# One straight program for each expert, with small conditional parts, in place of three arms

## The chip, the cores and the metric

The kernel runs on one core of a Trainium2 chip. The metric is the device time of one execution in microseconds (us). Each engine (TensorE, VectorE, ScalarE, GpSimd, SyncE) has an instruction stream of its own, and they wait for one another by semaphores. [...]

## What is computed

One layer on 256 tokens of 1024 channels: three token mixers, then a mixture of 32 experts of which each token takes four. The change touches the experts alone:

```python
def _moe(t, router_w, router_b, w_gu, b_gu, w_dn, b_dn):
    logits = (t @ router_w + router_b).astype(jnp.float32)
    top_vals, top_idx = lax.top_k(logits, TOP_K)
    gates = jax.nn.softmax(top_vals, axis=-1).astype(t.dtype)
    ...
    def expert_block(args):
        xe, e = args
        h = xe @ w_gu[e] + b_gu[e]
        gate, up = h[:, :D_FF], h[:, D_FF:]
        gate = jnp.minimum(gate, SWIGLU_LIMIT)
        up = jnp.clip(up, -SWIGLU_LIMIT, SWIGLU_LIMIT)
        return ((up + 1) * (gate * jax.nn.sigmoid(SWIGLU_ALPHA * gate))) @ w_dn[e] + b_dn[e]
```

Each expert holds 1024 x 2048 gate/up weights and 1024 x 1024 down weights in 32-bit floats, 12 MiB. How many tokens an expert has is known only when the kernel runs. With the inputs used here three experts (2, 15, 17) have over 64 tokens (84 at most), ten (3, 6, 7, 10, 12, 18, 24, 25, 30, 31) have 33 to 64, and the other nineteen 32 or fewer.

## The kernel before

The mixers run up to about 400 us, then the 32 experts one after another, then the final normalisation. Each expert's weights are twelve tiles of 1 MiB, `wt[0]` to `wt[7]` for gate/up (one for each 128 input channels) and `wt[8]` to `wt[11]` for down. They are loaded by SyncE into a ring of 19 slots, each as soon as the tile that held the slot has been read for the last time; the first 19 are loaded while the mixers still run.

The tokens of an expert are picked out of the 256 by a matmul with a one-hot matrix (`gather`), transposed to channels on partitions (`spread_rows`), multiplied with the weights, and put back by a second one-hot matmul (`scatter`, with the one-hot `sc` that VectorE makes from `pbr`) whose result VectorE adds to the accumulator `acc` (L1126). The product of the down weights is first multiplied with the gate (`weigh`: ScalarE L1115 makes the rounded part `yh`, then VectorE L1116 the rest `yl`). Two jobs are shared between neighbouring experts. `flush(prev)` is the scatter of the expert before: eight matmuls into four tiles, four additions. `fill` prepares the tokens of the next pair of experts, 64 places for each: an even expert gathers them (eight matmuls), an odd one transposes them (eight transposes).

An expert is one of three arms, chosen by its count in registers that each engine loads (L1294) and compares (L1337, L1338):

- `tiny`, up to 32 tokens: four groups of 32 array columns work side by side on four quarters of a weight tile (`pGU..t`, L1178 bias, L1183 gate/up, L1191 down bias, L1203 down).
- `light`, 33 to 64: two groups of 64 columns (L1139 bias, L1144 gate/up, L1162 down).
- `heavy`, over 64: a gather of its own for 128 places (L966) and all 128 columns (L1239, L1265).

In `tiny` and `light` TensorE's order is that of the code. After the second weight tile (`if k == 1`) stands the flush for an even expert and the transposes of fill for an odd one; after the down bias, beside the gate chain (`swiglu`: VectorE L1079, ScalarE L1081, VectorE L1083 to L1085), stands the other of the two. Then follow the turn of the gate product (`turned`, L1092, ScalarE L1094) and the down matmuls. Small results lie in four PSUM buffers with one tag (`sm`). Ahead of the last expert, 31, stands a jump (L1329) over code for experts with over 128 tokens, which doesn't run here, and an early flush of expert 30.

Of the kernel before, what the change touches and what calls it, by code (L numbers as in the profile page):

```python
# [29 lines left out]
TINY = 32  # L30
LIMIT = 7.0
# [109 lines left out]
def _consts():  # L141
# [26 lines left out]
    slot = np.full((P, 6), -5.0)  # L168
    slot[:64, 0] = p[:64] + 1
    slot[64:, 1] = p[:64] + 1  # L170
    slot[:, 2] = p + 1
    slot[:, 3] = p + 1 + P
    slot[:64, 4] = p[:64] % TINY + 1
    slot[64:, 5] = p[:64] % TINY + 1
# [8 lines left out]
def tile_trunk(ctx, tc, xT_d, xn_d, wf_d, vec_d, row_d, rw_d, cst_d, cst2_d, rope_d, ln1_d, ln2_d,  # L183
# [688 lines left out]
    cnt = mo.tile([P, NE + 1], I32, name="cnt")  # L872
    idr = mo.tile([P, P], F32R, name="idr")
# [122 lines left out]
    with tc.manual_schedule():  # L996
# [41 lines left out]
        V.tensor_copy(cnt[96:P, 0:NE], prk[1][96:P])  # L1038
        cmx = ch.tile([P, 1], F32, name="cmx")
# [30 lines left out]
    def sm(name, shape=None):  # L1070
        return pse.tile(shape or [P, 512], F32, tag="sm", name=name, bufs=4)

    def quarter(w, h, q):

        return w.rearrange("p (g n) -> p g n", g=2)[:, :, h * 512 + q * 256:h * 512 + (q + 1) * 256]

    def swiglu(ps, name):
# [4 lines left out]
        uv = ex.tile([P, 256], F32, tag="uv", name=f"uv{name}", bufs=2)  # L1082
# [14 lines left out]
    def gate_slots(lhs, e, name):  # L1097
# [6 lines left out]
        gsl = ex.tile([P, 1], F32, tag="gsl", name=f"gsl{name}", bufs=2)  # L1104
# [3 lines left out]
    def scatter_lhs(e, slots, sc, name):  # L1108
        pbr = sm(f"pbr{name}", [P, S])
        T.matmul(pbr, idr[:, e:e + 1].to_broadcast([P, P]), rankT, start=True, stop=True)  # L1110
        for i, s_ in enumerate(slots):
            V.tensor_scalar(sc[:, i], pbr, C("slot", s_, s_ + 1), None, op0=ALU.is_equal)  # L1112
# [5 lines left out]
    def scatter(c, n, sc, ys, name):  # L1118
        po = sm(f"pos{name}{c}{n}")
        ls = sc[:, c * P:(c + 1) * P]  # L1120
        w = 512 // len(ys)
        for i, (yh, yl) in enumerate(ys):
            T.matmul(po[:, i * w:(i + 1) * w], ls, yh, start=True, stop=False)  # L1123
            T.matmul(po[:, i * w:(i + 1) * w], ls, yl, start=False, stop=True)  # L1124
# [3 lines left out]
    def flush(prev):  # L1128
        if prev:
            e, sc, yh, yl = prev  # L1130
            for c in range(2):
                for n in range(2):
                    scatter(c, n, sc[:, n], [(yh, yl)], f"{e}")

    def light(e, oh, xg, bl, wt, prev, cur, fill):
        s_ = slice((e % 2) * CAP, (e % 2 + 1) * CAP)
        ps = [bank(2 + q, f"pGU{e}{q}") for q in range(2)]
        for q in range(2):
            T.matmul(ps[q], bl, bgu_t[:, q * 512:(q + 1) * 512], start=True, stop=False)  # L1139
        _, sc, yh, yl = cur  # L1140
        for k in range(KT):
            for q in range(2):
                for h in range(2):
                    T.matmul(ps[q][h * 64:(h + 1) * 64].rearrange("p (g n) -> p g n", g=2), xg[:, k, s_],  # L1144
                             quarter(wt[k], h, q), start=False, stop=(k == KT - 1))
            if k == 1:
                fill("l") if e % 2 else flush(prev)
            if k == 5:
                gsl = gate_slots(lambda c: oh[:, c, e % 2], e, f"{e}")
        pY = bank(0, f"pY{e}")  # L1150
        T.matmul(pY, bl, bdn_t, start=True, stop=False)
        uv = [swiglu(ps[q], f"{e}_{q}") for q in range(2)]
        flush(prev) if e % 2 else fill("l")
        scatter_lhs(e, (0, 1), sc, f"{e}")
        pT = bank(1, f"pT{e}", [P, 2, 2, P])
        hT = [turned(uv[q], f"{e}_{q}", pT[:, q]) for q in range(2)]
        for b in range(2):
            for h in range(2):
                for j in range(2):
                    lhs = hT[b][:, j, h * CAP:(h + 1) * CAP]  # L1160
                    for n in range(2):
                        T.matmul(pY[n * 64:(n + 1) * 64], lhs, wt[KT + 2 * b + h][:, j, n * 512:(n + 1) * 512],  # L1162
                                 start=False, stop=(b == 1 and h == 1 and j == 1))
        weigh(pY, gsl, yh, yl)

    def tiny(e, oh, xg, bl, wt, prev, cur, fill):


        nm = f"{e}t"
        ps = bank(2, f"pGU{nm}")  # L1170
        quarters = [(h, q) for h in range(2) for q in range(2)]
        _, sc, yh, yl = cur

        def grp(t, g):
            return t[g * TINY:(g + 1) * TINY]

        for g, (h, q) in enumerate(quarters):
            T.matmul(grp(ps, g), bl[:, g * TINY:(g + 1) * TINY].bitcast(F32),  # L1178
                     bgu_t[:, q * 512:(q + 1) * 512].bitcast(F32), start=True, stop=False)
        lo = (e % 2) * CAP  # L1180
        for k in range(KT):
            for g, (h, q) in enumerate(quarters):
                T.matmul(grp(ps, g).rearrange("p (g n) -> p g n", g=2), xg[:, k, lo:lo + TINY],  # L1183
                         quarter(wt[k], h, q), start=False, stop=(k == KT - 1))
            if k == 1:
                fill("t") if e % 2 else flush(prev)
            if k == 5:
                gsl = gate_slots(lambda c: oh[:, c, e % 2, 0:TINY], e, nm)
        pY = bank(0, f"pY{nm}")
        for n in range(2):  # L1190
            T.matmul(grp(pY, 2 * n), bl[:, n * CAP:n * CAP + TINY].bitcast(F32), bdn_t.bitcast(F32),  # L1191
                     start=True, stop=False)
        uv = swiglu(ps, nm)
        flush(prev) if e % 2 else fill("t")
        scatter_lhs(e, (4, 5), sc, nm)
        hT = turned(uv, nm, bank(1, f"pT{nm}", [P, 2, P]))
        for b in range(2):
            for h in range(2):
                g = 2 * h + b
                last_ = (b, h) == (1, 1)  # L1200
                for j in range(2):
                    for n in range(2):
                        T.matmul(grp(pY, 2 * n + j), hT[:, j, g * TINY:(g + 1) * TINY],  # L1203
                                 wt[KT + 2 * b + h][:, j, n * 512:(n + 1) * 512],
                                 start=(j == 1 and (b, h) == (0, 0)), stop=last_)
        weigh(pY, gsl, yh, yl)

    def heavy_onehot(e, part):
        oh = ex.tile([P, 2, P], F32R, tag=("ohx", "sg")[part], name=f"ohx{e}h{part}", bufs=2)
        for c in range(2):  # L1210
            V.tensor_scalar(oh[:, c], C("iota_s"), rank[c][:, e:e + 1], -float(part * P),
# [3 lines left out]
    def heavy_gather(e, part, ohx):  # L1215
# [5 lines left out]
        for i in range(4):  # L1221
            r = ex.tile([P, 256], F32, tag=("gv", "uv")[i % 2], name=f"raw{nm}{i}", bufs=2)
# [4 lines left out]
    def heavy(e, part, ohx, wt, prev, cur, fill=None):  # L1227
        nm = f"{e}h{part}"
        if fill and e % 2:
            fill("h")  # L1230
# [6 lines left out]

        def gu(k, h, q):
# [263 lines left out]
```

## Time and profile before

| | us |
|---|---|
| median of three runs | 1440.43 (1439.58 to 1445.16) |
| the profiled execution | 1446.26 |
| its span | 1444.4 |
| TensorE busy | 1139.7 (79%) |
| VectorE busy | 622.1 (43%) |
| ScalarE busy | 322.8 (22%) |
| GpSimd busy | 294.1 (20%) |

The span counts from the first to the last instruction of the profiled execution. Busy time says what an engine spent in operations, not what held up the end; for that one reads what an engine waited for and where its idle time lies. "Issue" as a releaser means that the engine waited for nothing that the profile shows, and an engine's name with a q stands for its sequencer, which handles branches and semaphores.

### The profile page before, as it was taken

The page shows a single profiled execution, that of the slowest core. Times are in us where ns is not written, and L with a number is a line of the kernel's source. Part 1 is how long each engine was busy: PE and PEld are TensorE (multiplying, and loading weights), DVE is VectorE, ACT ScalarE, POOL GpSimd, SP SyncE. Part 2 cuts the span into 40 slices and gives each one's busy share as a digit, 9 for nine tenths or more (in the row PEclk, how much of TensorE's full clock was granted, in tenths as well). Part 3 has the DMA queues.
Part 4 walks back from the last instruction along what each step waited for, and adds up shares of the span by engine and source line. Part 5 has one row for each costly group of instructions (what it writes and reads, how often), then busy time and mean ns, then how long its engine had stood idle before and what let it go on. Part 6 is the DMA issues. An engine that isn't in the chain of part 4 may idle for free. (4 is left out here: it accounts for less than half of the span.)

```text
span 1444.4 us, 18035 instructions
## 1 busy us (share of the span) xinstructions
PE 1139.7 (79%) x6902; PEld 635.4 (44%) x6902; DVE 622.1 (43%) x1289; ACT 322.8 (22%) x651; POOL 294.1 (20%) x293
## 2 busy tenths in 40 slices
PE   8797696899965998778597859869978678766666
PEld 8686586899722442233132325334322233221223
DVE  5999996876642232224222323313232312232203
ACT  5465463654411111011010101111100101100001
POOL 5999999533120000000000000000000000000000
PEclk9998788999888999899798979979999989999778
DMA  7243333477869689999999999966999999999950
GB/s 248 100 146 117 113 133 108 159 237 271 334 234 415 262 341 413 415 415 413 415 415 416 414 413 409 363 260 262 416 413 415 415 415 415 414 414 416 415 231 29
DMA packets 89524, 456.79 MB, mean 316 GB/s; under 512 B 8304, under 2 KB 8704, under 8 KB 58496
## 3 DMA queue, kind: packets, MB, share of 16 engines
q1 hardware_dynamic: 89344, 454.33, 79.6%
q8 instruction: 120, 1.97, 0.6%
q14 instruction: 60, 0.49, 0.1%
HBM read 453.25 MB, written 1.05 MB: 315 GB/s over the span
## 5 line engine op out<-in xcount | busy, mean ns | idle before, releaser
L1391 POOL TENSOR_TENSOR xn<-xn,lb 128x256 f32<-128x256 f32 x4 | 2.8, 726 | 1027.1 <-DVE xn L1379 1027.1
L1144 PE MATMUL pGU<-ew,xg 128*64 128x512 f32 x640 | 159.4, 649 | 0.7 <-issue 0.7
L1126 DVE TENSOR_TENSOR xn<-xn,pos 128x512 f32<-128x512 f32 x124 | 77.1, 680 | 134.0 <-issue 116.1
L393 POOL TENSOR_TENSOR cbc<-cbc,ups 128x256 f32<-128x256 f32 x120 | 123.4, 1029 | 4.6
L248 DVE TENSOR_TENSOR wl<-raw,wh 128x1024 fp32r<-128x1024 f32 (+1 forms) x72 | 99.9, 1394 | 37.3 <-ACT wh L247 37.1
L247 ACT CAST wh<-raw 128x1024 fp32r<-128x1024 f32 (+1 forms) x89 | 91.0, 1030 | 57.0 <-DMA raw<-in_wf_dram 23.4
L392 POOL TENSOR_TENSOR ups<-ups,vec 128x256 f32<-128x256 f32 x120 | 102.2, 871 | 0.0
L1144 PEld LDWEIGHTS pGU<-ew,xg 128*64 128x64 f32 x640 | 46.7, 149 | 95.9 <-issue 94.2
L1162 PE MATMUL pY<-ew,hT 128*64 128x512 f32 x320 | 75.1, 624 | 0.0
L1139 PE MATMUL pGU<-bgu_t,bl 128*128 128x512 f32 x20 | 10.9, 643 | 75.4 <-issue 74.7
L1081 ACT ACTIVATE sg<-gv 128x256 f32<-128x256 f32 x20 | 8.3, 417 | 224.2 <-DVE gv L1079 224.2
L1123 PE MATMUL pos<-yh,sc 128*128 128x512 f32 x124 | 52.8, 426 | 1.7 <-DVE yl L1116 1.7
L248 POOL TENSOR_TENSOR wl<-raw,wh 128x1024 fp32r<-128x1024 f32 x17 | 42.2, 2488 | 52.1 <-ACT wh L247 40.5
L1124 PE MATMUL pos<-yl,sc 128*128 128x512 f32 x124 | 48.8, 394 | 0.0
L1162 PEld LDWEIGHTS pY<-ew,hT 128*64 128x64 f32 x320 | 23.1, 144 | 45.1 <-issue 44.4
L1116 DVE SCALAR_TENSOR_TENSOR yl<-pY,gsl,yh 128x512 fp32r<-128x512 f32 x10 | 7.5, 750 | 80.4 <-ACT yh L1115 80.4
L1139 PEld LDWEIGHTS pGU<-bgu_t,bl 128*128 128x128 f32 x20 | 4.6, 287 | 82.7 <-issue 82.7
L1123 PEld LDWEIGHTS pos<-yh,sc 128*128 128x128 f32 x124 | 23.3, 188 | 29.0 <-issue 21.9
L403 DVE SCALAR_TENSOR_TENSOR xacc<-xp,vec,xacc 128x256 f32<-128x256 f32 x48 | 35.6, 746 | 0.5
L1105 DVE COPY gsl<-pgs 128x1 f32<-128x1 f32 x10 | 1.6, 158 | 76.8 <-PE pgs L1103 76.8
L291 PE MATMUL px<-xh,wh 128*128 128x256 f32 x96 | 29.9, 312 | 5.9 <-ACT pt L553 4.8
L293 PE MATMUL px<-xh,wl 128*128 128x256 f32 x96 | 28.9, 301 | 0.4 <-DVE wl L248 0.4
(1235 smaller groups left out, 2567.4 us busy)
## 6 DMA issues: line engine op xcount, KB each, us to landing
ew<-in_wgu_dram SPq DMA_DIRECT2D x241, 1024.0 KB, 19.9
ew<-in_wdn_dram SPq DMA_DIRECT2D x124, 1024.0 KB, 19.4
raw<-in_wf_dram SPq DMA_DIRECT2D x87, 512.0 KB, 3.6
ew<-in_wgu_dram SPq DMA_DIRECT2D x30, 512.0 KB, 6.3
ew<-in_wdn_dram SPq DMA_DIRECT2D x8, 512.0 KB, 5.7
xraw<-in_xT_dram SPq DMA_DIRECT2D x4, 256.0 KB, 5.1
xn<-in_xn_dram SPq DMA_DIRECT2D x2, 512.0 KB, 6.7
lnt<-in_ln_dram SPq DMA_DIRECT2D x2, 512.0 KB, 10.1
```

What stands on the lines that cost most here:

```text
L247: A.copy(h[:, b], raw[:, b])
L248: (PO if u in LOW_POOL else V).tensor_sub(l[:, b], raw[:, b], h[:, b].bitcast(F32))
L291: T.matmul(ps, wh, mh(k), start=(k == 0), stop=False)
L293: T.matmul(ps, wl, mh(k), start=False, stop=(k == nk - 1))
L392: PO.tensor_tensor(pr, up[:, j:j + S], W("cw31", c * 31 + j).to_broadcast([P, S]), op=ALU.mult)
L393: PO.tensor_add(acc, acc, pr)
L403: V.scalar_tensor_tensor(acc, xp[:, j:j + S], W("cw5", t * 5 + j), acc, op0=ALU.mult, op1=ALU.add)
L1123: T.matmul(po[:, i * w:(i + 1) * w], ls, yh, start=True, stop=False)
L1124: T.matmul(po[:, i * w:(i + 1) * w], ls, yl, start=False, stop=True)
L1126: V.tensor_add(dst, dst, po)
L1144: T.matmul(ps[q][h * 64:(h + 1) * 64].rearrange("p (g n) -> p g n", g=2), xg[:, k, s_], quarter(wt[k], h, q), start=False, stop=(k == KT - 1))
L1162: T.matmul(pY[n * 64:(n + 1) * 64], lhs, wt[KT + 2 * b + h][:, j, n * 512:(n + 1) * 512], start=False, stop=(b == 1 and h == 1 and j == 1))
```

## The change

The three arms give way to one function, `expert`. Each expert is now up to two groups: `many` is true over 32 tokens and runs the first 64 places as two groups of 64 columns, `four` is true up to 32 and over 64 and runs one group of 32 places as four groups of 32 columns (the expert's only tokens, or places 65 to 96), `over` is true over 64. The flags are computed on VectorE for all experts at once; each engine loads three of them into registers for each expert. The work is cut into parts, each in a conditional of its own: the second gather, gate/up of two weight tiles at a time, the gate chain, the turn, down of two weight tiles at a time, the middle scatter, and the weighting. On TensorE these are 18 conditionals for an expert, on ScalarE and VectorE nine each. A part that is left out is a taken branch to one instruction that waits until TensorE (or the engine it is on) has finished all that stands ahead, and then raises the engine's semaphore by the part's count.

The scatter takes 64 of the 128 partitions for each half of the channels and one scatter one-hot in place of two. The small PSUM tiles have three buffers in place of four. The fallback now covers experts with over 96 tokens (`TOP`), which do not occur here, and stays as a jump ahead of expert 31.

```diff
+    flag = mo.tile([P, 3, NE], I32, name="flag")
+    base = mo.tile([P, NE], F32, name="base")
...
+        pn = mm("pn", [P, NE])
+        for c in range(2):
+            T.matmul(pn, C("ones"), Pm[c], start=(c == 0), stop=(c == 1))
+        V.tensor_scalar(base, pn, float(CAP), float(CAP), op0=ALU.is_gt, op1=ALU.mult)
+        V.tensor_scalar(flag[:, 0], pn, float(TINY), None, op0=ALU.is_gt)
+        V.tensor_scalar(flag[:, 1], pn, float(CAP), None, op0=ALU.is_gt)
+        V.scalar_tensor_tensor(flag[:, 2], pn, float(TINY), flag[:, 1], op0=ALU.is_le, op1=ALU.add)
...
     def sm(name, shape=None):
-        return pse.tile(shape or [P, 512], F32, tag="sm", name=name, bufs=4)
+        return pse.tile(shape or [P, 512], F32, tag="sm", name=name, bufs=3)
...
+    def scatter(pos, c, sc, ys, start=True):
+
+        for i, y in enumerate(ys):
+            for n in range(2):
+                r = slice(n * 64, (n + 1) * 64)
+                T.matmul(pos[n], sc[r, c * P:(c + 1) * P], y[r], start=(start and i == 0), stop=(i == 1))
...
+    def expert(e, oh, xg, bl, wt, prev, cur, fill):
+
+
+        many, over, four = [[nc.values_load(flag[0:1, i, e:e + 1], engines=g, min_val=0, max_val=1,
+                                            skip_runtime_bounds_check_because="comparisons of a count")
+                             for g in ((ENG.PE,), (ENG.Activation, ENG.DVE))] for i in range(3)]
...
+        first, second = (fill, lambda: flush(prev)) if e % 2 else (lambda: flush(prev), fill)
+
+        def on(cond, *parts):
+
+            for c_, f in zip(cond, parts):
+                if f:
+                    with tc.If(c_):
+                        with pe_order():
+                            f()
...
+        xs_ = ex.tile([P, KT, TINY], F32, tag="xsm", name=f"xsm{e}", bufs=1)
+        A.copy(xs_, xg[:, :, lo:lo + TINY])
+        pg = bank(1, f"pgs{e}", [P, KT, TINY])
...
+        on(over, gather_more, copy_more)
+        pL = [bank(2 + q, f"pGL{e}{q}") for q in range(2)]
+        pS = bank(4, f"pGS{e}")
+
+        def up_many(k0):
...
+            for k in (k0, k0 + 1):
+                for q in range(2):
+                    for h in range(2):
+                        T.matmul(pL[q][h * 64:(h + 1) * 64].rearrange("p (g n) -> p g n", g=2),
+                                 xg[:, k, s_], quarter(wt[k], h, q), start=False, stop=(k == KT - 1))
+
+        def up_four(k0):
...
+            for k in (k0, k0 + 1):
+                for g, (h, q) in enumerate(QUARTERS):
+                    T.matmul(grp(pS, g).rearrange("p (g n) -> p g n", g=2), xs_[:, k],
+                             quarter(wt[k], h, q), start=False, stop=(k == KT - 1))
+
+        for k0 in range(0, KT, 2):
+            on(many, lambda: up_many(k0))
+            on(four, lambda: up_four(k0))
+            if k0 == 0:
+                with pe_order():
+                    first()
+        uv = [gate_tiles(f"{e}_{q}") for q in range(2)]
+        on(many, None, lambda: [swiglu_into(uv[q], pL[q]) for q in range(2)])
+        uv.append(gate_tiles(f"{e}_2"))
+        on(four, None, lambda: swiglu_into(uv[2], pS))
+        with pe_order():
+            second()
...
+        on(many, turn_many, turned_many)
+        on(four, turn_four, turned_four)
...
         for b in range(2):
+            on(many, lambda: down_many(b))
+            on(four, lambda: down_four(b))
+        on(many, None, lambda: weigh(pY[0], gsl[0], yh, yl))
+        for c in range(2):
+            pos = [sm(f"pom{e}{c}{n}") for n in range(2)]
+            on(over, lambda: scatter(pos, c, sc, (yh, yl)), lambda: [add(c, n, pos[n]) for n in range(2)])
+        pb2 = sm(f"pbs{e}", [P, S])
+        on(four, lambda: T.matmul(pb2, idr[:, e:e + 1].to_broadcast([P, P]), rankT, start=True, stop=True),
+           lambda: (slots(sc, pb2, 1, e), weigh(pY[1], gsl[1], yh, yl)))
...
-            with tc.If(count(NE, ALL) > P):
+            with tc.If(count(NE, ALL) > TOP):
...
-        rv = count(e, (ENG.PE, ENG.Activation, ENG.DVE))
-        with tc.If(rv > TINY) as some:
-            with tc.If(rv > CAP) as cond:
-                heavy(e, 0, ohx, wt, prev, cur, fill)
-            with cond.Else():
-                with tc.manual_schedule(engines={mybir.EngineType.PE}):
-                    light(e, oh, xg, bl, wt, prev, cur, fill)
-        with some.Else():
-            with tc.manual_schedule(engines={mybir.EngineType.PE}):
-                tiny(e, oh, xg, bl, wt, prev, cur, fill)
+        expert(e, oh, xg, bl, wt, prev, cur, fill)
```

The order of the built program differs from that of the code in one respect: what stands in the code after the first gate/up parts is scheduled, from expert 4 on, ahead of them. On TensorE, the start of expert 20, an even one with up to 32 tokens, read before as follows (`pos` is the flush, `pGU20t` gate/up):

```order
L1294 TENSOR_LOAD cnt
L1337 COMPARE_AND_BRANCH
L1178 MATMUL pGU20t<-bgu_t,bl_13835 32x512 [waits PE_49]
L1183 MATMUL pGU20t<-ew_20_0_14317,xg_13324 32x512 [waits DMAHW3_49]
L1183 MATMUL pGU20t<-ew_20_1_14319,xg_13324 32x512 [waits DMAHW4_49]
L1123 MATMUL pos_14699<-yh,sc 128x512 [waits DVE_49,PE_49,Activation_49]
L1124 MATMUL pos_14699<-yl,sc 128x512
L1123 MATMUL pos_14703<-yh,sc 128x512 [waits PE_49]
L1183 MATMUL pGU20t<-ew_20_2_14321,xg_13324 32x512 [waits DMAHW5_49]
```

The same place of the changed kernel on TensorE (`pGL` is the gate/up of 64 places, `pGS` that of 32, `pgx` the gather of fill):

```order
L1183 UNCONDITIONAL_BRANCH [waits PE_49]
L1150 MATMUL pos_13231<-yh,sc 128x512 [waits DVE_49,PE_49,Activation_49]
L1150 MATMUL pos_13231<-yl,sc 128x512 [waits DVE_49]
L1150 MATMUL pos_13240<-yh,sc 128x512 [waits DVE_49]
L963 MATMUL pgx_13355<-nh,ohp_13091 128x512 [waits DVE_49]
L1183 COMPARE_AND_BRANCH
L1213 MATMUL pGL_13196<-bgu_t,bl_12682 128x512
L1217 MATMUL pGL_13196<-ew_20_0_13095,xg_12228 64x512 [waits DMAHW3_49]
L1183 UNCONDITIONAL_BRANCH [waits PE_49]
L1223 MATMUL pGS_13198<-bgu_t,bl_12682 32x512 x4
L1227 MATMUL pGS_13198<-ew_20_0_13095,xsm_13145 32x512 [waits DMAHW3_49,Activation_49]
```

The flush and the gather moved from behind the second weight tile, and from beside the gate chain, to the front of the expert, and between two stretches of gate/up of the group of 32 stands the left-out part of the group of 64 with its wait.

Between gate/up and down of the same expert TensorE's row read before (`pY20t` the down bias, `pgx20t` the gather, `pT20t` the turn):

```order
L1191 MATMUL pY20t<-bdn_t,bl_13835 32x512 x2
L966 MATMUL pgx20t_14761<-nh,ohp_14313 128x512 [waits DVE_49]
L966 MATMUL pgx20t_14762<-nl,ohp_14313 128x512
L1110 MATMUL pbr20t<-rankT,idr 128x256 [waits DVE_49]
L1092 MATMUL pT20t<-cst,uv20t 128x128 [waits DVE_49]
L1203 MATMUL pY20t<-ew_20_8_14333,hT20t 32x512 [waits DMAHW3_49,Activation_49]
```

and in the changed kernel:

```order
L1183 UNCONDITIONAL_BRANCH [waits PE_49]
L1183 COMPARE_AND_BRANCH
L1097 MATMUL pgs_13370<-Gm_4244,ohs_13142 32x1 [waits DVE_49]
L1266 MATMUL pY_13368<-bdn_t,bl_12682 32x512 [waits PE_49,Activation_49]
L1269 MATMUL pTS_13373<-cst,uv_2_13342 128x128 [waits DVE_49,PE_49]
L1308 MATMUL pY_13368<-ew_20_8_13111,hT_13376 32x512 [waits DMAHW3_49,PE_49,Activation_49]
```

The gather and `pbr` no longer stand between the down bias and the turn; the gate column came there, and the wait of the left-out turn of the group of 64 stands ahead.

## Rows read from the trace of the kernel before

**Rows 1.** The page: span, TensorE's busy time and share, GB/s moved in 40 slices.

```profile
span 1444.4 us, 18035 instructions
...
PE 1139.7 (79%) x6902; PEld 635.4 (44%) x6902; DVE 622.1 (43%) x1289; ACT 322.8 (22%) x651; POOL 294.1 (20%) x293
...
GB/s 248 100 146 117 113 133 108 159 237 271 334 234 415 262 341 413 415 415 413 415 415 416 414 413 409 363 260 262 416 413 415 415 415 415 414 414 416 415 231 29
```

**Rows 2.** The page's DMA issues: count, KB each, median us to landing.

```profile
ew<-in_wgu_dram SPq DMA_DIRECT2D x241, 1024.0 KB, 19.9
ew<-in_wdn_dram SPq DMA_DIRECT2D x124, 1024.0 KB, 19.4
```

**Rows 3.** TensorE's waits, 400 to 1420 us: total us, times, longest.

```profile
PE pGU L1139 <- issue: 74.7, 8, 12.7
PE pgt15h L980 <- issue: 16.0, 1, 16.0
PE pgx2h L966 <- issue: 15.0, 1, 15.0
PE pgt17h L980 <- issue: 14.8, 1, 14.8
```

**Rows 4.** Line L1178, tiny bias: ns min/median/max, first and last start; idle before.

```profile
L1178 PE MATMUL pGU0t<-bgu_t,bl x8: 1033/1061/1062, 405.2 to 406.0; 128*32 128x512 f32 x8
...
L1178 PE MATMUL pGU13t<-bgu_t,bl x8: 592/604/617, 807.5 to 808.0; 128*32 128x512 f32 x8
...
L1178 PE MATMUL pGU19t<-bgu_t,bl x8: 1033/1061/1062, 1035.9 to 1036.7; 128*32 128x512 f32 x8
...
  issue: 57.1, 13
```

**Rows 5.** Branches of the arms (L1337) and of the fallback (L1329), by engine.

```profile
L1337 PEldq COMPARE_BRANCH  x51: 69/5304/6818, 396.6 to 1389.2; - x51
...
L1337 DVEq COMPARE_BRANCH  x51: 43/50/63, 409.9 to 1391.0; - x51
L1337 SPq COMPARE_BRANCH  x32: 33/33/38, 385.8 to 1391.4; - x32
...
L1329 PEldq EVENT_SEMAPHORE  x2: 51/51/51, 1388.5 to 1388.6; - x2
...
L1329 PEldq COMPARE_BRANCH  x1: 4735/4735/4735, 1383.7 to 1383.7; - x1
```

**Rows 6.** Line L1203, tiny down: ns min/median/max, first and last start.

```profile
L1203 PE MATMUL pY13t<-ew,hT13t x32: 592/592/617, 820.5 to 823.6; 128*32 128x512 f32 x32
...
L1203 PE MATMUL pY19t<-ew,hT19t x32: 592/592/617, 1050.5 to 1053.5; 128*32 128x512 f32 x32
```

**Rows 7.** Timeline of TensorE, expert 8: start, us, operation, idle before.

```profile
675.19 1.03 PE L1191 MATMUL pY8t<-bdn_t,bl 128*32 128x512 f32 x4
...
679.39 0.44 PE L1092 MATMUL pT8t<-cst,uv8t 128*128 128x128 f32 x2 [1.00 <-DVE uv8t L1085]
680.36 3.64 PE L1203 MATMUL pY8t<-ew,hT8t 128*32 128x512 f32 x32 [0.53 <-ACT hT8t L1094]
```

**Rows 8.** Timeline of TensorE at experts 3, 30 and 31.

```profile
536.40 7.09 PE L1162 MATMUL pY<-ew,hT 128*64 128x512 f32 x32
...
1370.10 0.55 PE L1092 MATMUL pT<-cst,uv 128*128 128x128 f32 x2 [2.10 <-DVE uv L1085]
...
1371.80 9.70 PE L1162 MATMUL pY<-ew,hT 128*64 128x512 f32 x32
1383.24 0.47 PE L1123 MATMUL pos<-yh,sc 128*128 128x512 f32 x1 [1.73 <-DVE yl L1116]
...
1418.26 8.67 PE L1162 MATMUL pY<-ew,hT 128*64 128x512 f32 x32
```

**Rows 9.** The page's groups by line: busy us, mean ns, idle before.

```profile
L1126 DVE TENSOR_TENSOR xn<-xn,pos 128x512 f32<-128x512 f32 x124 | 77.1, 680 | 134.0 <-issue 116.1
...
L1081 ACT ACTIVATE sg<-gv 128x256 f32<-128x256 f32 x20 | 8.3, 417 | 224.2 <-DVE gv L1079 224.2
```

More of the change, by code (lines that the diff above doesn't have):

```diff
@@ L30 @@
 TINY = 32
+TOP = CAP + TINY
 LIMIT = 7.0
@@ L1116, in weigh, with add @@
         V.scalar_tensor_tensor(yl, pY, gsl, yh.bitcast(F32), op0=ALU.mult, op1=ALU.subtract)
[L1118 to L1124, printed above, removed]
+    def scatter(pos, c, sc, ys, start=True):
[3 more added lines that the diff above has]
+                T.matmul(pos[n], sc[r, c * P:(c + 1) * P], y[r], start=(start and i == 0), stop=(i == 1))
+    def add(c, n, po):
         dst = acc[:, c, n * 512:(n + 1) * 512]
@@ L1131, in flush @@
             for c in range(2):
+                pos = [sm(f"pos{e}{c}{n}") for n in range(2)]
+                scatter(pos, c, sc, (yh, yl))
                 for n in range(2):
[L1133 to L1139, printed above, removed]
-        _, sc, yh, yl = cur
-        for k in range(KT):
-            for q in range(2):
[L1143 to L1157, printed above, removed]
@@ L1166, in tiny @@
[L1166 to L1196, printed above, removed]
-        for b in range(2):
[L1198 to L1206, printed above, removed]
@@ L1225, in heavy_gather, with heavy @@
         spread_rows(xgx, lambda k: rows[k // 2][:, k % 2 * P:(k % 2 + 1) * P], nm)
-    def heavy(e, part, ohx, wt, prev, cur, fill=None):
+    def heavy(e, part, wt, cur):
         nm = f"{e}h{part}"
-        if fill and e % 2:
-            fill("h")
+        ohx = heavy_onehot(e, part)
         heavy_gather(e, part, ohx)
@@ L1236, in heavy @@
             T.matmul(ps[h, q], bls[h], bgu_t[:, q * 512:(q + 1) * 512], start=True, stop=False)
-        def gu(k, h, q):
-            T.matmul(ps[h, q].rearrange("p (g n) -> p g n", g=2), xgx[:, k], quarter(wt[k], h, q),
-                     start=False, stop=(k == KT - 1))
-        for k in range(6):
+        for k in range(KT):
             for h, q in qs:
-                gu(k, h, q)
-            if k == 1:
-                flush(prev)
+                T.matmul(ps[h, q].rearrange("p (g n) -> p g n", g=2), xgx[:, k], quarter(wt[k], h, q),
+                         start=False, stop=(k == KT - 1))
@@ new lines, in heavy @@
+        hT = {hq: turned(swiglu(ps[hq], f"{nm}_{hq[0]}{hq[1]}"), f"{nm}_{hq[0]}{hq[1]}") for hq in qs}
+        for n in range(2):
+            pY = bank(n, f"pY{nm}{n}")
+            T.matmul(pY, bls[n], bdn_t, start=True, stop=False)
+            for b in range(2):
+                for h in range(2):
+                    for j in range(2):
+                        T.matmul(pY, hT[h, b][:, j], wt[KT + 2 * b + h][:, j, n * 512:(n + 1) * 512],
+                                 start=False, stop=(b == 1 and h == 1 and j == 1))
+            weigh(pY, gsl, yh, yl)
+            for c in range(2):
+                po = sm(f"pos{nm}{c}{n}")
+                for i, y in enumerate((yh, yl)):
+                    T.matmul(po, sc[:, c * P:(c + 1) * P], y, start=(i == 0), stop=(i == 1))
+                add(c, n, po)
@@ L1308, in tile_trunk, with fill @@
                         onehot(ohn, c, e + 2)
-        def fill(arm, e=e, more=more):
+        def fill(arm="", e=e, more=more):
             if more and e % 2 == 0:
@@ L1356, in total, with add1 @@
             for n in range(2):
-                pz[c][n] = sm(f"pz{c}{n}")
+                pz[c][n] = bank(4, "pz11") if c and n else sm(f"pz{c}{n}")
                 if c == 0:
                     T.matmul(pz[c][n], C("ident"), acc[:, c, n * 512:(n + 1) * 512], start=True, stop=False)
-            for n in range(2):
-                for i, y in enumerate((yh, yl)):
-                    T.matmul(pz[c][n], sc[:, n, c * P:(c + 1) * P], y, start=(c == 1 and i == 0), stop=(i == 1))
-        def add(n):
+            scatter(pz[c], c, sc, (yh, yl), start=(c == 1))
+        def add1(n):
             dst = acc[:, 1, n * 512:(n + 1) * 512]
```

168 lines of the change are left out of this document (106 added, 62 removed).

## The prediction

> **What bounds the kernel now.** I read the page first: a span of 1444.4 us, TensorE busy 79% of it, and in the last 30 of 40 slices weights arriving at up to 416 GB/s, with dips only where the three experts with over 64 tokens run [rows 1]. The reader is to see two limits there that lie close together. The weights: 241 and 124 transfers of 1 MiB are issued while the experts run [rows 2], and at 415 GB/s one takes 1048576 / 415000 = 2.53 us, so 365 of them take 922 us. TensorE: the first expert starts at 405 us [rows 4] and the last one's down work ends at 1418.3 + 8.7 = 1427 us [rows 8], 17 us before the end, so TensorE spends 1022 us on the experts, 100 more than their transfers need. TensorE is thus the later of the two, and next I asked what it waits for. The answer is "issue", nothing the profile shows as a releaser: 74.7 us in 8 waits ahead of the 33-to-64-token arm, 57.1 us in 13 ahead of the up-to-32-token arm, and 16.0, 15.0 and 14.8 us ahead of the three over-64 arms [rows 3, 4], together 177.6 us. The branch rows say what it is: on TensorE's sequencer a compare-and-branch takes 69 ns at best, but 5304 ns in the median, while on VectorE and SyncE the same branches take 50 and 33 ns [rows 5]. A jump over another arm costs TensorE some 5 us; a tiny arm ends in one, and an entry to a light arm is one.
>
> **What the change removes.** (a) Those waits: 177.6 us. The jump over the fallback at the last expert stays, and its branch took 4.7 us [rows 5]; I leave 6 us for it. Removed: 171.6 us. (b) After such a wait TensorE runs at its lower level for a while: the bias matmuls of expert 19 take 1061 ns, those of expert 13 take 604 [rows 4]. From the first bias matmul to the last down matmul expert 13 takes 823.6 - 807.5 = 16.1 us and expert 19, with the same work, 1053.5 - 1035.9 = 17.6 us [rows 4, 6]: 1.5 us an entry. With 13 tiny, 8 light and 3 heavy entries that follow a wait: 36 us. Removed in all: 208 us.
>
> **What it adds, at full clock, for each expert.** (c) Flush and fill now stand ahead of all gate/up parts, so the flush waits for the weighting of the expert just ended. Before, two weight tiles of work lay between. The trace shows this wait bare once, at the last expert, where the fallback forces an early flush: 1.73 us of idle [rows 8]. Some branches and register loads lie in it, so I take 2.2 us for even experts; for odd ones the eight transposes (1.1 us) fill half of it: 1.65 us in the mean. (d) The small PSUM tiles go from four buffers to three, so the fourth accumulation and the gather behind it wait for additions of 680 ns [rows 9]: first add done at about 0.7 + 0.7 us after the flush starts, while the fourth tile is wanted at 1.2, and the gather waits for the second and third in the same way. 1.45 us for even and 0.65 for odd, 1.05 in the mean. (e) The gate chain of the expert (four operations of a quarter tile on VectorE and one on ScalarE, each about as long as ScalarE's 417 ns [rows 9]) was covered by flush or fill and the down bias: expert 8 ends its up work at 675.2 and starts its down work at 680.4 with idle gaps of only 1.00 and 0.53 us [rows 7]. Now only the gate column and the down bias lie there (0.5 to 0.9 us), and about 1.5 us more stand idle: 1.5 for tiny, 1.6 for light. (f) Every part that is left out becomes a taken branch and a wait for all earlier TensorE work. No row of before shows a short jump over a part, so it is bounded: below by a jump that costs nothing beyond the drained pipeline, the 592 ns of a last matmul [rows 6] less its own slot of 0.11 (3.64 us for 32 in expert 8 [rows 7]), or 0.48 us less what overlaps, say 0.35; above by the 5.3 us of [rows 5]. I take 0.48 + 0.05 for the semaphore row + 0.07 for the not-taken branch that follows [rows 5], rounded up to 0.65 us, because the jump itself can be passed while queued matmuls still run, and because the parts are a tenth of an arm in length. Ten parts are left out in a tiny expert, but those at its end, at the gate chain and ahead of the flush fall into waits already counted; four are bare, as are four in a light expert: 2.6 us.
>
> A tiny expert gains 1.65 + 1.05 + 1.5 + 2.6 = 6.8 us of work and waits, a light one 6.9. The three heavy experts now run a group of 64 and one of 32 instead of one of 128: their gate/up and down matmuls fall from four full banks to two and one, but they have a second gather, a second turn and a scatter in the middle that waits for its weighting. By the same rows I make it 3 us longer each. Sum: 19 x 6.8 + 10 x 6.9 + 3 x 3 = 129 + 69 + 9 = 207 us.
>
> What I cost at nothing: the count flags (four VectorE operations and two small matmuls beside the ranking; they are over before the first bias matmul, which waits for ScalarE); the two extra register loads an expert, passed while the flush is queued; the 32-token copy on ScalarE, which is idle 224 us ahead of a single group of its operations [rows 9]; SyncE's branches, at 33 ns each [rows 5], some 50 to the expert, 1.7 us of a queue that issues 12 transfers in 30 us and lies 19.9 us ahead of landing [rows 2]. If that cover is gone each of these shows as a wait on a transfer or on ScalarE.
>
> **The sum.** Against the profiled execution: 1446 - 208 + 207 = 1445 us. The median of the runs shown is 1440.4, 5.8 below that execution, so the sum gives about 1440; I put 1445, since (f) is more likely too low than too high. An error of 0.35 us in (f) alone, up or down, is 4 x 29 x 0.35 = 40 us, so this case spans 1415 to 1465.
>
> **Rivals.** *Faster: the drains are nearly free.* With 0.35 us for (f), and with the four-buffer waits of (d) hidden because half-height scatters for two banks overlap, 35 + 15 us go: 1390 us. For it: the 177.6 us of stalls are real, and the transfers would permit 100 us less. Against it: no row shows TensorE restarting within 0.35 us. It cannot go below about 1340, where the 922 us of transfers decide. *Slower: TensorE loses its clock in the new gaps.* At experts 30 and 31 the gate chain is uncovered already; at expert 30 the idle before the transposes is 2.10 us, and the 32 down matmuls behind it take 9.70 us, and at expert 31 8.67, instead of the 7.09 at expert 3 [rows 8]: 2.6 and 1.6 us lost. After gaps of 1.00 us [rows 7] nothing is lost. The new gaps, (c) 1.7 to 2.2 us and (e) 2 to 2.5 us, lie between those. If one an expert brings the lower level, at the 1.5 us of (b), that is 29 x 1.5 = 44 us: 1485. It decides from gaps of about 2 us on, at the down matmuls and at the first bias matmuls. *Slower by far: the short jumps stall too.* TensorE passes 18 branches an expert. If one or two of them find their target not yet there, each costs 5.3 us less the work queued ahead, about 4 us of idle (the 57.1 us in 13 waits give 4.4): 32 x 4 = 128 us or more, 1570. For it: the change then doesn't do what it says, and nothing in the trace shows a short jump. Against it: the fastest branches, 69 ns, are there too, and a skipped part is some ten matmuls.
>
> [...]
>
> **How the numbers follow.** Break-even as summed, 1415 to 1465: 0.40. Drains nearly free, 1385 to 1415: 0.20. Clock lost once an expert, 1465 to 1515: 0.29. Short jumps that stall: 0.08. Something else: 0.03. What a measurement of this kernel can tell from no change is about 0.5%, or 1433 to 1448. Of the break-even case 0.14 lies below that, 0.13 inside and 0.13 above. So faster 0.35, same 0.13, slower 0.52. The range leaves out the fetch rival and the ends of the first two rivals: 1392 to 1515.
>
> **What would show it.** In the profile after, TensorE's waits on "issue" ahead of bias matmuls should shrink from 4 to 15 us each to under 1 us each, but be some ten times as many; a wait on VectorE's weighting or ScalarE's should stand ahead of each flush (1.7 to 2.2 us) and one on VectorE's gate product ahead of each turn (1.3 to 2 us). [...] The bias matmuls' median, 604 or 1061 ns, and the granted clock by slice tell whether the clock rival holds. If the weights come at 415 GB/s without dips to the end, the transfers have become the bound and I was wrong on the low side. The prediction would be wrong in its base if a tiny expert takes under 23 us or over 29 us from start to start.

## The result, and the profile of the changed kernel

The changed kernel takes 1501.8 us in the median (1495.9 to 1502.7) against 1442.8 for the kernel before in the same sessions: a ratio of 1.039, 95% interval 1.035 to 1.044. It is slower, inside the range and on the side that had 0.52, but 57 us above the forecast of 1445. The page of its profiled execution, span, TensorE's busy time, granted clock and GB/s in 40 slices, answers to [rows 1]:

```profile
span 1500.5 us, 22214 instructions
...
PE 1194.4 (80%) x7326; PEld 626.5 (42%) x7326; DVE 616.0 (41%) x1249; ACT 327.5 (22%) x668; POOL 293.9 (20%) x293
...
PEclk9998797999795988999898897989989899988877
...
GB/s 235 107 154 110 108 142 114 167 254 279 222 320 354 301 278 384 415 392 385 416 417 404 359 414 352 248 330 295 334 372 412 416 416 416 413 415 416 343 234 29
```

The span grew by 56.1 us and TensorE's busy time by 54.7, from 1139.7. Its idle time stayed what it was: 304.7 us before, 306.1 after. So the waits that came are as long as those that went (the sum had 207 us of work and waits coming against 171.6 us of waits going, and made up the difference with the clock), and the loss lies in the time that TensorE's work takes. The clock record of both traces (PEclk) has two values, 1.0 and 0.5 of full speed, called the upper and the lower level here; sixteen down matmuls take 1.92 us at the upper (1130.33 us, expert 20) and 3.64 at the lower (458.58 us, expert 1). Summing TensorE's matmul time over the stretches at the lower level, from 400 us on, gives 114 us before and 224 after. Reckoned at the recorded 1.0 in place of 0.5 that work takes half as long, so the lower level costs 57 us before and 112 after: 55 us more, as much as the whole loss. Of 802 and 856 us of matmul time from 405 us on, that leaves 802 - 57 = 745 and 856 - 112 = 744 us of work reckoned at the upper level, the same in both. These are balances of the whole: what each part of the change costs or saves is left to the runs below.

The branches of the parts on TensorE (ns, min/median/max), against [rows 5]:

```profile
L1183 PEldq COMPARE_BRANCH  x852: 63/176/3778, 398.7 to 1481.8; - x171
```

The median fell from 5304 to 176 ns: the stalls of the long jumps are gone. The one branch of 3.8 us stands in expert 31, behind the fallback's jump, which itself takes 6.8 us; TensorE waits 11.9 us there. What TensorE waits for instead (total us, times, longest), against [rows 3]:

```profile
PE pGS L1227 <- PEq L1183: 20.0, 50, 0.7
PE pos L1150 <- DVE xg L969: 16.5, 15, 2.7
PE pbs L1298 <- PEq L1183: 16.5, 19, 1.1
PE pgt L977 <- PEq L1183: 16.4, 11, 2.7
PE pTS L1269 <- DVE gsl L1272: 16.1, 19, 1.3
PE pos L1150 <- PEq L1183: 15.3, 12, 2.6
PE pos L1150 <- DVE xn L1154: 14.0, 30, 2.2
PE pGS L1223 <- PEq L1183: 12.4, 17, 0.8
PE pGL L1213 <- PEq L1171: 11.9, 1, 11.9
```

Many short waits stand in place of 24 long ones; L1183 is the conditional. How they lie is seen in the timeline of expert 20 and the start of 21, both with up to 32 tokens (start, us, operation, idle before); `pos` is the flush, `pgx` the gather of fill, `pGS` gate/up, `pTS` the turn:

```profile
1109.31 0.35 PE L1298 MATMUL pbs<-rankT,idr 128*128 128x256 f32 x1 [0.87 <-PEq L1183]
1110.49 0.50 PE L1150 MATMUL pos<-yh,sc 64*128 64x512 f32 x2 [0.82 <-PEq L1183]
...
1112.23 0.50 PE L1150 MATMUL pos<-yh,sc 64*128 64x512 f32 x1 [0.55 <-DVE xn L1154]
...
1113.08 1.24 PE L963 MATMUL pgx<-nh,ohp 128*128 128x512 f32 x2
1114.12 1.05 PE L963 MATMUL pgx<-nl,ohp 128*128 128x512 f32 x2
...
1117.28 1.07 PE L1223 MATMUL pGS<-bgu_t,bl 128*32 128x512 f32 x8 [0.72 <-PEq L1183]
1118.15 1.91 PE L1227 MATMUL pGS<-ew,xsm 128*32 128x512 f32 x16
1120.51 1.92 PE L1227 MATMUL pGS<-ew,xsm 128*32 128x512 f32 x16 [0.45 <-PEq L1183]
...
1127.51 0.44 PE L1097 MATMUL pgs<-Gm,ohs 128*32 128x1 f32 x16 [0.34 <-PEq L1183]
...
1129.27 0.41 PE L1269 MATMUL pTS<-cst,uv 128*128 128x128 f32 x2 [0.37 <-DVE gsl L1272]
1130.33 1.92 PE L1308 MATMUL pY<-ew,hT 128*32 128x512 f32 x16 [0.65 <-ACT hT L1273]
1132.69 1.92 PE L1308 MATMUL pY<-ew,hT 128*32 128x512 f32 x16 [0.45 <-PEq L1183]
...
1142.67 1.94 PE L1223 MATMUL pGS<-bgu_t,bl 128*32 128x512 f32 x8 [0.72 <-PEq L1183]
1144.37 3.09 PE L1227 MATMUL pGS<-ew,xsm 128*32 128x512 f32 x16
```

Two things are to be seen. A left-out part costs what was reckoned: gate/up pieces start 1120.51 - 1118.15 = 2.36 us apart where sixteen matmuls more in one row take 1.72 (32 take 3.64 [rows 7], 16 take 1.92), so 0.64. And the clock: after the thin stretch at the front, in which no gap is longer than 0.9 us, the gather's matmuls take 0.43 us each (four from 1114.12 to 1115.83 us), where expert 8's in the kernel before took 0.23 (six from 676.72 to 678.12), and the next expert starts its gate/up at the lower level as well (3.09 us for sixteen instead of 1.92).

From the first gate/up matmul of one expert (that of the bias) to that of the next, the seventeen tiny experts (up to 32 tokens) from 4 on take 474 us against 483 before, the nine light ones (33 to 64) ahead of 31 340 against 301, the three heavy ones 153 against 149, experts 0 and 1 68 against 60, expert 31 31 against 29. The experts start 9.5 us later, and the tail is 2.3 us longer. Of the 110 us more at the lower level, 65 lie in the tiny experts, 24 in the heavy and 16 in the first two; the nine light ones have 45 us before and after, and what they lost is idle time. The loss is therefore not the clock's alone.

### The profile page after: what moved, and what is told of

It reads as the page before. It is cut to its first block, busy times and chain, and to the rows that moved or that the text cites. A ratio compares the mean times of both kernels' runs of the same rounds, so it can differ in the third digit from the quotient of the medians.

```text
span 1500.5 us, 22214 instructions
## 1 busy us (share of the span) xinstructions
PE 1194.4 (80%) x7326; PEld 626.5 (42%) x7326; DVE 616.0 (41%) x1249; ACT 327.5 (22%) x668; POOL 293.9 (20%) x293
## 3 DMA queue, kind: packets, MB, share of 16 engines
HBM read 453.25 MB, written 1.05 MB: 303 GB/s over the span
## 5 line engine op out<-in xcount | busy, mean ns | idle before, releaser
L1217 PE MATMUL pGL<-ew,xg 128*64 128x512 f32 x832 | 198.0, 619 | 10.2 <-PEq L1183 9.5
L1227 PE MATMUL pGS<-ew,xsm 128*32 128x512 f32 x1408 | 180.4, 634 | 20.8 <-PEq L1183 20.0
L1217 PEld LDWEIGHTS pGL<-ew,xg 128*64 128x64 f32 x832 | 59.2, 142 | 143.6 <-issue 133.1
L1227 PEld LDWEIGHTS pGS<-ew,xsm 128*32 128x32 f32 x1408 | 46.5, 117 | 156.7 <-issue 146.4
L1282 PE MATMUL pY<-ew,hT 128*64 128x512 f32 x416 | 99.7, 622 | 10.4 <-ACT hT L1261 4.9
L1308 PE MATMUL pY<-ew,hT 128*32 128x512 f32 x704 | 90.2, 631 | 21.3 <-PEq L1183 11.0
L1150 PE MATMUL pos<-yh,sc 64*128 64x512 f32 x124 | 66.4, 622 | 51.1 <-DVE xg L969 16.5
L1142 ACT ACTIVATE yh<-pY,gsl 128x512 fp32r<-128x512 f32 x35 | 24.0, 687 | 218.3 <-PEq L1183 111.7
L1150 PEld LDWEIGHTS pos<-yh,sc 64*128 64x128 f32 x124 | 26.5, 235 | 83.3 <-DVE xn L1154 29.9
L1150 PE MATMUL pos<-yl,sc 64*128 64x512 f32 x124 | 58.8, 611 | 0.0
```

The lines of the kernel that those rows point to most:

```text
L1142: A.activation(yh, pY, AF.Copy, scale=gsl)
L1150: T.matmul(pos[n], sc[r, c * P:(c + 1) * P], y[r], start=(start and i == 0), stop=(i == 1))
L1217: T.matmul(pL[q][h * 64:(h + 1) * 64].rearrange("p (g n) -> p g n", g=2), xg[:, k, s_], quarter(wt[k], h, q), start=False, stop=(k == KT - 1))
L1227: T.matmul(grp(pS, g).rearrange("p (g n) -> p g n", g=2), xs_[:, k], quarter(wt[k], h, q), start=False, stop=(k == KT - 1))
L1282: T.matmul(pY[0][n * 64:(n + 1) * 64], hT[b][:, j, h * CAP:(h + 1) * CAP], wt[KT + 2 * b + h][:, j, n * 512:(n + 1) * 512], start=False, s ...
```

## The experiments

Two theories stood against each other: the waits of left-out parts, and the order that puts flush and fill at the front, with the clock that falls there. Times are medians; the kernel before measured 1439.5 to 1442 beside them, and 1442.8 beside the changed kernel, so a difference of 3 us between runs of different sessions says nothing.

**The order of the code on TensorE.**

```diff
-        expert(e, oh, xg, bl, wt, prev, cur, fill)
+        with pe_order():
+            expert(e, oh, xg, bl, wt, prev, cur, fill)
```

> TensorE's instructions of each expert are kept in the order of the code, conditionals included: flush (or transposes) behind the first two weight tiles, the other of the two beside the gate chain. Theory: the loss of the changed kernel (1502 against 1443) is that flush and fill at the front leave the weighting and the gate chain bare, and that TensorE then works 224 us at its lower clock level against 114 before. Then about 3 us of waits an expert and most of the extra 110 us at the lower level go: 1502 - 32 x 3 - 40 = 1365 to 1400, with the lower level back under 150 us. Rival, the drained skips are the loss (0.65 us each, as measured between two gate/up parts): these stay, and the time falls by no more than the waits that the rows show ahead of the flush, some 30 to 40 us: 1460 to 1475.

Measured: 1493.8 us, 8 less than the changed kernel, of which some 3 lie between the sessions; neither number came. Lower-level work fell to 199 us only. TensorE's waits show why:

```profile
PE pGS L1223 <- PEq L1183: 48.0, 17, 3.9
PE pos L1150 <- DVE xn L1154: 35.5, 31, 2.1
PE pGL L1213 <- PEq L1183: 25.3, 10, 5.7
```

The first bias matmuls now wait 48.0 + 25.3 us where they had waited 12.4 and, at the fallback alone, 11.9: the last conditionals of one expert, three register loads and the first conditionals of the next take some 2.4 us, which the flush's own wait had hidden. Expert 20 in the timeline:

```profile
1103.52 1.67 PE L1223 MATMUL pGS<-bgu_t,bl 128*32 128x512 f32 x8 [2.44 <-PEq L1183]
```
The flush still waits for the additions, 35.5 us against 14.0. So the weighting's wait was no cost of its own: moving the flush away from it lays bare the seam of conditionals.

**Parts of eight weight tiles, and parts of one.** Edits of the two loops (`k0` in steps of 8 or 1 with as many tiles to a part), in the first also one part for all down work.

```diff
-        for k0 in range(0, KT, 2):
+        for k0 in range(0, KT, 8):
...
-        for b in range(2):
-            on(many, lambda: down_many(b))
-            on(four, lambda: down_four(b))
+        on(many, lambda: [down_many(b) for b in range(2)])
+        on(four, lambda: [down_four(b) for b in range(2)])
```

> Order as in the changed kernel, but gate/up is one part of eight weight tiles and down one of four: 10 TensorE conditionals an expert instead of 18. Theory of the drains at 0.65 us: three fewer bare drains in gate/up and one in down, 4 x 0.65 x 29 experts with one group = 75 us less, 1427, or less by what the clock takes. [...]

> The reverse: gate/up in eight parts of one weight tile each, down as in the changed kernel: four more drained skips in each expert with one group. At 0.65 us each 4 x 0.65 x 29 = 75 us more: 1575. If the drains are hidden or the clock is what counts, within 15 us of 1502 (more gaps of under half a us only).

Measured: 1452.3 us with large parts, 49.5 less, and 1543.4 with small ones, 41.6 more. In the kernel with large parts, the branch row, and gate/up and down of expert 21 in the timeline:

```profile
L1183 PEldq COMPARE_BRANCH  x456: 63/176/443, 397.9 to 1434.8; - x152
```

```profile
1084.45 8.33 PE L1227 MATMUL pGS<-ew,xsm 128*32 128x512 f32 x64
...
1095.92 3.64 PE L1307 MATMUL pY<-ew,hT 128*32 128x512 f32 x32 [0.64 <-ACT hT L1273]
```

No branch of the parts takes over 443 ns although it now jumps 34 matmuls, or 72 where the group of 32 is left out: jumps of this length do not stall either. Down takes 3.64 us in one piece, 1.92 + 0.45 + 1.92 in two. The slope is 0.36 us a left-out part in the one direction (41.6 / 116) and 0.43 in the other, less than 0.64: part of it is paid back, by the transfers (with large parts TensorE waits for them again, 8.4 us at down) and by the clock (lower-level work 254 us with large parts, 210 with small). Reckoned at the upper level TensorE's work is 717 us with large parts (844 - 254 / 2), 27 less than in the changed kernel: of the 0.64 us, 0.45 stand as idle time and the rest within the work, which is thus the same before and after only by balance. So the left-out parts are a real cost of some 45 us, which the next runs set beside that of the front.

**Four small PSUM buffers.**

```diff
-        return pse.tile(shape or [P, 512], F32, tag="sm", name=name, bufs=3)
+        return pse.tile(shape or [P, 512], F32, tag="sm", name=name, bufs=4)
...
-        pS = bank(4, f"pGS{e}")
+        pS = bank(1, f"pGS{e}")
...
-        pTS = bank(4, f"pTS{e}", [P, 2, P])
+        pTS = bank(3, f"pTS{e}", [P, 2, P])
...
-                pz[c][n] = bank(4, "pz11") if c and n else sm(f"pz{c}{n}")
+                pz[c][n] = sm(f"pz{c}{n}")
```

> The small PSUM tiles have four buffers again: the gate/up result of the group of 32 moves to the bank of the second gather, its turned result to the bank of the second gate/up result. Order and parts as in the changed kernel. If the wait for the additions counts as predicted, 1.05 us in the mean for 31 flushes: 1502 - 33 = 1469, and the clock may give back some more. If DVE's additions would only hold up the next tile instead, within 10 us of 1502.

Measured: 1455.1 us, 47 less; I had 33. Experts 20 and 21 in the timeline:

```profile
1087.97 0.50 PE L1150 MATMUL pos<-yh,sc 64*128 64x512 f32 x2 [0.82 <-PEq L1183]
1088.45 0.50 PE L1150 MATMUL pos<-yl,sc 64*128 64x512 f32 x2
1088.79 0.39 PE L1150 MATMUL pos<-yh,sc 64*128 64x512 f32 x2
1089.02 0.39 PE L1150 MATMUL pos<-yl,sc 64*128 64x512 f32 x2
...
1118.58 1.07 PE L1223 MATMUL pGS<-bgu_t,bl 128*32 128x512 f32 x8 [0.71 <-PEq L1183]
1119.45 1.91 PE L1227 MATMUL pGS<-ew,xsm 128*32 128x512 f32 x16
```

The flush runs through without a wait for an addition, and expert 21's gate/up starts at the upper level: 1.91 us for sixteen where the changed kernel took 3.09. Lower-level work fell from 224 to 165 us, worth 30 of the 47 us; the other 17 are about what the wait itself costs in the kernel before (18.7 us, below). Three results changed their PSUM banks with the edit; what that does by itself was not tried.

**The clock by itself.** A first attempt, with idle matmuls written to a tile of their own:

```diff
+                wm = bank(4, f"wm{e}{c}", [P, S])
+                for _i in range(5):
+                    T.matmul(wm, idr, rankT, start=True, stop=True)
                 pos = [sm(f"pos{e}{c}{n}") for n in range(2)]
                 scatter(pos, c, sc, (yh, yl))
```

> The changed kernel with ten idle matmuls of 256 columns more in each expert, five ahead of each half of the flush, whose results are not used (0.12 us each at full clock, 1.2 us an expert). Theory that a good part of the loss is the clock that falls in the thin stretch at the front of each expert: TensorE's work at the lower level falls from 224 us to under 150 and the time falls by 15 to 40 us although there is more to do. If the clock is only a companion: 0 to 36 us more, 1502 to 1538.

Measured: 1532.9 us. It decides nothing: the new tile shares a bank with gate/up and moved the flush behind it, beside the gate chain, so that order and filling changed together. The second attempt writes them into the tile that the flush starts anew:

```diff
                 pos = [sm(f"pos{e}{c}{n}") for n in range(2)]
+                for _i in range(5):
+                    T.matmul(pos[0][:, 0:S], idr, rankT, start=True, stop=True)
                 scatter(pos, c, sc, (yh, yl))
```

> The changed kernel with ten matmuls of 256 columns more in each expert whose results are overwritten: five at the head of each half of the flush, written into the tile that the flush then starts anew, so that no tile and no order changes (the run e7_warm had moved the flush behind gate/up, which made it a test of something else). At full clock they are 10 x 0.115 = 1.15 us an expert, and stand where TensorE waits for the weighting and for the additions anyway. If the clock that falls at the front of the expert is a cause, the work at the lower level drops clearly under 224 us and the time by 10 to 40 us in spite of 36 us of added work. If the clock only goes with the gaps, or these matmuls just delay the flush: the same or up to 36 us more.

Measured: 1488.3 us, 13.5 less than the changed kernel, with 31 x 10 matmuls more to do. As a ratio to the kernel before beside each it is 1.032 (1.028 to 1.036) after 1.039 (1.035 to 1.044): the intervals overlap slightly, but the executions do not (1486.4 to 1491.6 us against 1495.9 to 1502.7), and the granted clock is higher in each, 0.908 to 0.911 against 0.878 to 0.884. The mean granted clock of the changed kernel's profiled execution, and of this one's:

```profile
core 0: 1500.5 us, clock 0.880
```

```profile
core 0: 1485.6 us, clock 0.911
```

Its expert 21 in the timeline:

```profile
1137.42 1.07 PE L1225 MATMUL pGS<-bgu_t,bl 128*32 128x512 f32 x8 [0.81 <-PEq L1185]
1138.29 1.91 PE L1229 MATMUL pGS<-ew,xsm 128*32 128x512 f32 x16
```

It starts gate/up at the upper level again, and lower-level work falls to 162 us, 31 us less at the cost of it. That the time falls when work is added is not to be had from waits alone: the clock is a cause, not a companion.

**The kernel before with three buffers.**

```diff
-        return pse.tile(shape or [P, 512], F32, tag="sm", name=name, bufs=4)
+        return pse.tile(shape or [P, 512], F32, tag="sm", name=name, bufs=3)
```

> The kernel before with three small PSUM buffers in place of four and nothing else changed. In its order flush stands behind two weight tiles or beside the gate chain, so the fourth accumulation waits for the first addition there too, some 0.6 us, and the gather behind it: if the cost lies in the additions alone, 31 x 1 = 20 to 35 us more (1460 to 1475). If it needs the flush at the front to cost, under 10 us.

Measured: 1459.3 us, 18.7 more (ratio 1.014, 1.012 to 1.015), just under the lower figure. Lower-level work is 117 us, against 114. So 0.6 us a flush is what the fourth buffer is worth where the flush stands amid other work; at the front it is worth two and a half times that, through the clock.

**Both edits, with and without the order.**

> Both edits that each took some 50 us off the changed kernel (gate/up in one part and down in one part; four small PSUM buffers). If they work on different waits, the drains inside gate/up and the front of the expert, they add: 1502 - 50 - 47 = 1405, faster than the kernel before (1440). If both work through the same thing, the level of TensorE's clock, the second gives less: 1430 to 1450.

> As the run with both edits, and TensorE in the order of the code: flush (or transposes) behind all of gate/up, the other beside the gate chain. The order alone gave 8 us, since what it covered at the gate chain it laid bare at the seam of two experts (the register loads and left-out parts there) and at the additions. With four buffers the additions no longer count: 20 to 30 us less than the same without the order, 1375 to 1385, if the seam of 3.5 us is the only loss; the same 1405, within 10, if the seam gives back all.

> The version with gate/up and down in one part each and four small PSUM buffers (1429.5), and TensorE in the order of the code for experts 0 and 1 alone. There the fill's gather stands ahead of the first gate/up and waits 13.5 us for VectorE, and the second expert's matmuls wait in the same way; with the whole kernel ordered the third expert started 10 us earlier. If these waits are the start's loss, 8 to 10 us less: 1420. If the end is set by the transfers, which move at 415 GB/s from expert 18 on, less: 1425 to 1430.

Measured: 1429.5 us with large parts and four buffers, a ratio to the kernel before of 0.992 (0.991 to 0.994), so faster than both kernels, than the kernel before by 0.8%; 1451.0 with the order of the code in addition; 1429.2 with that order for experts 0 and 1 alone (0.990, 0.988 to 0.993). The first falls short of 1405, and the page and TensorE's waits of it say what took over:

```profile
GB/s 247 103 148 121 114 135 103 148 229 282 345 120 415 252 284 381 414 415 416 415 416 415 413 416 417 416 398 283 262 415 415 415 415 414 415 416 415 415 349 159
```

```profile
PE pGS L1227 <- DMA ew<-in_wgu_dram: 23.9, 23, 1.5
...
PE pY L1307 <- DMA ew<-in_wdn_dram: 11.0, 8, 2.0
```

From the slice after the last heavy expert the transfers run at 415 GB/s until they end, and TensorE waits 35 us for them. Lower-level work is still 203 us, 89 more than in the kernel before, which is slower all the same: where the transfers decide, that sum no longer tells the loss. With the order of the code flush and fill stand together beside a gate chain too short for both, the seam is bare, and lower-level work rises to 241 us: 21 us worse. The start, in the version with the order for two experts, isn't mended by it:

```profile
412.59 1.93 PE L1223 MATMUL pGS<-bgu_t,bl 128*32 128x512 f32 x8 [14.16 <-DVEq L1183]
```

VectorE gets to the first expert's conditional only after the gates and the next pair's one-hot, which ends at 411.8 us here, whichever matmul waits for it there, so my reading of that wait as a matter of TensorE's order was wrong.

## Why the prediction was right or wrong

The measured time lies inside the range and on the side held likeliest, but in the interval of the clock rival (1465 to 1515, 0.29) and not in that of the sum (0.40), which missed by 57 us. That the sum came no further off is in part luck, as the terms show. The interval of the sum was also too narrow by its own working: 40 us either way are 1405 to 1485, not 1415 to 1465.

*What bounds the kernel*: right. TensorE was the later of two close limits, and when it got faster the transfers decided, at 1429.

*(a), the stalls removed*: right; branch median 176 ns. The short jumps did not stall, nor did those over 34 or 72 matmuls (443 ns at most), but for single branches (the one of 3.8 us in expert 31, and one of 1.2 us in the run with large parts and four buffers). The range calls this rival the fetch rival; what a branch of 5.3 us spends its time on, no run shows. At expert 31 6 us were left for the fallback, and 11.9 came.

*(b), the clock given back*: this is the step that failed. I credited 36 us for lower-level stretches that end with the stalls. The stalls went, but the stretches came elsewhere: lower-level work rose by 110 us, a loss of 55 where a gain of 36 stood in the sum, 91 us in all. The clock rival had the mechanism, 44 us and 1485, but I put it beside the sum as a rival with 0.29 instead of taking the credit out of it; and I tied it to single gaps of about 2 us, from the 2.10 us of [rows 8]. Of the 36 falls of the clock within the experts ten come behind a gap of 2.3 to 2.7 us at the flush or the transposes, as the rival had it; at the other 26 no gap just ahead is longer than 1.5 us, at expert 20 none longer than 0.9. The sign that I had named for it, the median of the bias matmuls, would have misled:

```profile
L1223 PE MATMUL pGS<-bgu_t,bl x176: 589/617/1063, 414.7 to 1378.5; 128*32 128x512 f32 x176
```

The median is 617 ns, since twelve of the 22 groups of eight run at the upper level; before, six of 19 did. A tiny expert takes 27.9 us in the mean, inside the 23 to 29 named.

*(c) weighting's wait*: somewhat short (0.87 + 0.82 us idle ahead of expert 20's flush, but 2.1 us in the mean of all 31 seams of two experts, 1.65 forecast, some 14 us in all), and the place wrong: branches and register loads take that time anyhow, as the run with the order of the code showed.

*(d) three buffers*: 1.05 us forecast, 0.6 measured where nothing else depends on it, 1.5 here with the clock. Not credited was that the flush's matmuls themselves take some 1.3 us in place of 1.95 where no addition holds them up (last section): about 20 us over 31 flushes, an estimate.

*(e) the gate chain*: 1.5 us of new idle time forecast, 0.8 found in the mean. Expert 20, an even one, has 0.34, 0.37 and 0.65 us idle there, 1.4 together, against the 1.53 of [rows 7], so nothing new: without fill beside it the chain itself is shorter, 2.1 us from the end of gate/up to the turn (1127.2 to 1129.3) where it was 4.2 (675.2 to 679.4; there VectorE made fill's copy, 0.69 us from 678.3 on, ahead of the chain's last step). In the odd tiny experts, where the flush had covered the chain, the 1.5 us did come. Expert 1 before (turn and down), and expert 21 now (gate column, turn and down):

```profile
442.23 0.38 PE L1092 MATMUL pT1t<-cst,uv1t 128*128 128x128 f32 x2
443.14 3.64 PE L1203 MATMUL pY1t<-ew,hT1t 128*32 128x512 f32 x32 [0.53 <-ACT hT1t L1094]
```

```profile
1154.77 0.31 PE L1097 MATMUL pgs<-Gm,ohs 128*32 128x1 f32 x16 [0.40 <-PEq L1183]
...
1157.04 0.41 PE L1269 MATMUL pTS<-cst,uv 128*128 128x128 f32 x2 [1.08 <-DVE gsl L1272]
1157.98 1.92 PE L1308 MATMUL pY<-ew,hT 128*32 128x512 f32 x16 [0.53 <-ACTq L1183]
```

The light experts went from 0.5 to 0.8 us there to 1.5 to 1.6 (30 and 31, bare before, from 2.6). Over the 29 tiny and light experts the idle time between gate/up and down rose from 29 to 52 us: 23 where the sum had 44, which hid about a quarter of the error in (b).

*(f) the left-out parts*: 0.65 forecast, 0.64 in the rows, 0.36 to 0.43 net of clock and transfers. The heavy experts grew by 4 us in all, 9 forecast.

*What I cost at nothing*: the start was not free. The first expert's work begins at 414.7 us instead of 405.2, since its first matmuls wait for VectorE:

```profile
413.21 0.77 PE L963 MATMUL pgx<-nh,ohp 128*128 128x512 f32 x1 [13.55 <-DVEq L1183]
414.70 1.93 PE L1223 MATMUL pGS<-bgu_t,bl 128*32 128x512 f32 x8 [0.72 <-DVEq L1183]
```

## What to carry to other kernels

When long stalls are replaced by many short waits, add up TensorE's work at each clock level before and after, and not the idle time alone: here the idle time came out equal to 1.4 us, and the loss is as large as what the work at half speed costs more (55 us). Where the transfers decided, at 415 GB/s in the run of 1429.5 us, that sum no longer told the loss. Cut conditional work into few parts (each left-out one costs 0.64 us here, and the median jump, 176 ns, is the same over 34 matmuls as over 10), and keep the PSUM buffers that let a burst of small results run through (the fourth was worth 47 us here). Work that covers a wait may be covering two; before moving it, ask what else ends in the same place.

## What the runs showed of the hardware

That useless matmuls in waits can pay: 310 of them took 13.5 us off, by lifting the mean granted clock from 0.880 to 0.911. That the lower clock level came at experts 20 and 21 of the changed kernel after stretches in which no single gap was longer than 1.1 us, while at expert 8 of the kernel before a gap of 1.00 us amid dense work [rows 7] did nothing. And that scatter matmuls on the two halves of the partitions run side by side. In the run with four buffers a pair starts every 0.23 us (1088.79, 1089.02, above); on all 128 partitions, at expert 8 before, one starts every 0.23 us:

```profile
669.34 0.39 PE L1123 MATMUL pos<-yh,sc 128*128 128x512 f32 x1
669.57 0.39 PE L1124 MATMUL pos<-yl,sc 128*128 128x512 f32 x1
```

So the eight of a flush take 1.3 us there, 1087.97 to 0.23 us behind the last pair's start, and 1.95 at expert 8 (from 667.85). A version that mends the start was not tried.
